# A six-stage encoder trunk in fp32 pairs: from hand-set orders and rooms to one list schedule over shared rooms

## The chip, the cores and the metric

The kernel runs on one core of a Trainium2 chip. The metric is the device time of one execution in microseconds (us). TensorE is called PE, VectorE DVE, ScalarE ACT, GpSimd POOL, and SyncE, which here only issues loads, SP.

## The reference

256 tokens of 1024 features go through two layers, each of three blocks with a residual and a layer norm: a gated feed-forward network (FFN, 2816 hidden), a mixer, and another FFN. The mixer of layer 0 is a bidirectional mLSTM with four heads, that of layer 1 windowed attention with 16 query heads and 4 key heads. Weights and data are float32.

```python
def swiglu(x, w_in, w_out):
    gu = x @ w_in
    g, u = gu[..., :D_FF], gu[..., D_FF:]
    return (jax.nn.silu(g) * u) @ w_out

def reference(x, ...):
    for l in range(DEPTH):
        x = layer_norm(ALPHA * x + 0.5 * swiglu(x, ffn_w_in[l, 0], ffn_w_out[l, 0]), ln_g[l, 0], ln_b[l, 0])
        j = l // N_MIXERS
        if l % N_MIXERS == 0:
            y = mlstm_mixer(x, ml_w_in[j], ml_gate_b[j], ml_norm_g[j], ml_w_out[j])
        else:
            y = window_attention(x, at_w_in[j], at_sink[j], at_w_out[j])
        x = layer_norm(ALPHA * x + y, ln_g[l, 1], ln_b[l, 1])
        x = layer_norm(ALPHA * x + 0.5 * swiglu(x, ffn_w_in[l, 1], ffn_w_out[l, 1]), ln_g[l, 2], ln_b[l, 2])
    return x
```

## The kernel before

Each float32 operand of a product is split into a rounded part (hi) and the rest (lo), and a product is three matmuls: hi x hi, hi x lo, lo x hi (`mm3`, L545). Weights come as raw words of 128 x 1024 (512 KB). ACT casts a word into `w_hi`, DVE subtracts that from the word into `w_lo`, and both lie in a ring of ten tiles (RING) until PE has used them. The normalized x is kept transposed in `xT`, also as hi and lo.

An FFN (`ffn`, L689) goes through its 2816 columns in this order: 512 columns by plain products, for which eight words stay in the ring while token half 0 and then token half 1 is multiplied (the first FFN takes both halves word by word); 256 columns from four words that hold gate and up side by side; two down rows (words of `w_out`, 12 matmuls each); and four groups (`seven`, L862) of 512 columns, in which seven block products stand in for eight, as in Strassen's scheme. A group uses sums of x blocks (S1 to S4), and sums of weight blocks that are made in place: DVE adds one raw word to another, and POOL issues a load that adds a block from memory onto a word (`Weights.transfer`, L305). Between the products stand further down rows, 16 in all by the end of the groups. `tail` (L644) then takes the last six rows, first all for token half 0 and then for half 1; `Norm` (L601) follows on DVE, with the power -0.5 on POOL; and `emit_x` (L685) transposes the new x on PE, for half 0 within the tail and for half 1 (`pending`) some matmuls into the next stage.

What sets the order. The instructions of each engine are written out in Python in their final order, and each engine works through its own queue strictly in order, with semaphores between the queues.

- PE's order is the program's.
- In the FFN stages the order of splits and sums on ACT and DVE comes from `Paced` (L56), which keeps an estimated clock for PE, DVE, ACT and the DMA, and from `Weights.fill` (L324), which is called after each matmul and emits a split when its word is expected to be in memory by 1 us before that (SOON). Elsewhere, and in the tails, tables of counts say how many splits go between which steps: RS, PU, MP, PD, TD. EX, LC and SW order other steps.
- Loads are issued on SP by `Weights.load` (L187), whenever a raw room becomes free. There are four rooms `w_raw` for all words; the words of the groups have eight rooms `s_raw0` to `s_raw3` and one `v_raw` in the pool of the stage. `Weights.open` (L179), called as an FFN begins (L812; in the first FFN at L808), declares these free, and the loads that fit go out at once.
- PSUM has eight banks, four named `pw` and four `py`.

The instructions of all engines but POOL are recorded by one helper (L142), so the profile gives that line for most of them; L108 and L106 are the loads.

Of the kernel before, what the change touches and what calls it, by code (L numbers as in the profile page):

```python
# [1 line left out]

# [14 lines left out]
D = 1024  # L17
# [7 lines left out]
RAW_BUFS = 4  # L25
S_RAW = 2
TAGS = ("w_raw", "s_raw0", "s_raw1", "s_raw2", "s_raw3")
V_RAW = 1
RING = 10
PU = [2, 0, 1, 2, 1, 2, 1, 1, 0, 1, 2, 4]  # L30
QC = [2, 12, 20, 28, 32]
SW = 1
FB = [1, 0, 1, 0, 2, 0, 0, 0, 1, 1, 2]
CT = [0, 1]
EX = [1, 2, 2, 2, 2, 2, 2, 2]
RS = [0, 0, 1, 0, 1, 0, 0, 0, 0, 0, 0, 3, 0, 0, 1, 0, 1, 0, 1, 0, 0, 0, 2, 0, 0, 0, 1, 0, 1, 2, 0, 0, 0, 1, 0, 0, 2, 0, 1, 1, 0, 0, 0, 0, 2, 2, 0, 1]
XP = [4, 0, 1, 2]
LC = [0, 0, 0, 0, 0, 1]
TD = [2, 3, 2, 0, 2, 1]
MP = [1, 0, 0, 0, 1, 0, 1, 1, 0, 0, 0, 0, 2, 2, 2]  # L40
PD = [7, 0, 6, 6, 5]
PEND = [6, 4, 6, 6, 6]


AHEAD = 300.0
SOON = -1000.0
NEAR = -700.0
LOOK = 6
LANDING = 2200.0
LOADING = 1340.0  # L50
SECOND = 1250.0
ADDING = 7000.0
SHARE = 2500.0


class Paced:  # L56

    def __init__(self, nc):  # L60
        self.nc = nc
        self.pe = self.vec = self.act = self.dma = 0.0
        self.there, self.places = {}, {}
        self.filler, self.alone = None, True
        self.vector = Engine(nc.vector, self.on_vector)
        self.scalar = Engine(nc.scalar, self.on_scalar)
        self.tensor = Engine(nc.tensor, self.on_tensor)

    def __getattr__(self, name):
        return getattr(self.nc, name)  # L70

    def place(self, ap):

        f = ap.ap[0][0]
        key = (ap.offset % f if f else 0, tuple(ap.ap[1:]))
        if key not in self.places:
            i = np.array([key[0]])
            for step, n in key[1]:
                i = (i[:, None] + step * np.arange(n if step else 1)[None, :]).reshape(-1)
            self.places[key] = i  # L80
        return self.places[key]

    def when(self, *aps):
        t = 0.0
        for ap in aps:
            a = self.there.get(ap.name)
            if a is not None:
                i = self.place(ap)
                t = max(t, a[i[i < a.size]].max(initial=0.0))
        return t  # L90

    def mark(self, ap, t):
        i = self.place(ap)
        a = self.there.get(ap.name)
        if a is None or a.size <= i.max():
            self.there[ap.name] = np.zeros(int(i.max()) + 1)
            if a is not None:
                self.there[ap.name][:a.size] = a
        self.there[ap.name][i] = t

    def load(self, ap, source, engine=None):
        if engine is not None:
            engine.dma_start(ap, source)
        elif isinstance(source, list):
            for k, src in enumerate(source):
                self.nc.sync.dma_start(ap[:, k].rearrange("p (m f) -> p m f", m=src.shape[1]), src)  # L106
        else:
            self.nc.sync.dma_start(ap, source)  # L108
        come = self.pe + LANDING
        alone, self.alone = self.alone, come > self.dma  # L110
        self.dma = max(self.dma, come) + LOADING + (SECOND if alone and not self.alone else 0.0)
        self.mark(ap, self.dma)

    def on_vector(self, name, n, out, ins):
        self.vec = max(self.vec, self.when(*ins)) + (n + 71) / 0.96
        for o in out:
            self.mark(o, self.vec + 115)

    def on_scalar(self, name, n, out, ins):
# [1394 lines left out]
```

## Time and profile before

| | before |
|---|---|
| device time, median of 3 runs | 935.05 us |
| lowest and highest run | 929.75, 936.56 us |
| span of the profiled execution | 940.3 us |
| instructions | 12583 |
| moved by DMA | 208.53 MB |

The profiled execution has no time of its own beside its span, which runs from its first to its last instruction; it is 5.25 us longer than the median of the runs. In the profile a matmul's busy time includes the time in which it is on its way through the array, so that neighbours overlap; the interval between the starts of two matmuls says how fast PE goes. A row of a table of windows gives start and end, length, busy time and count for PE, its weight loads (PEld), DVE, ACT and POOL, the granted clock of PE, the share of time in which the DMA engines were busy, and GB/s. A row of the chain of waits gives start, length, and the work on which the end of the program hung in that time. "Idle before" names the last instruction that a waiting one waited for.

### The profile page before, as it was taken

How to read it: one execution, taken by the hardware profiler on the slowest of the kernel's cores; microseconds unless marked ns; L12 is line 12 of the kernel's file. 1: busy time of each engine (PE TensorE's matmuls, PEld its weight loads, DVE VectorE, ACT ScalarE, POOL GpSimd, SP SyncE). 2: the span in 40 equal slices, each digit the busy share in tenths (PEclk: the TensorE clock that was granted, in tenths of full speed). 3: DMA queues.
4: the chain of work that ended last, by engine and by line, in shares of the span. 5: the costliest groups of instructions: out<-in, count | busy, mean ns of one | idle time of the engine just before them, and what ended most of it. 6: DMA issues, size and time to landing. Idle time of an engine off the chain costs nothing.

```text
span 940.3 us, 12583 instructions
## 1 busy us (share of the span) xinstructions
PE 915.2 (97%) x4459; PEld 758.6 (81%) x4459; DVE 804.3 (86%) x969; ACT 569.1 (61%) x793; POOL 155.2 (17%) x194
## 2 busy tenths in 40 slices
PE   9999999999999999999999899999999999999997
PEld 7777878789988877887777688887888887888885
DVE  5879999986799798899985999998868887889996
ACT  5566666446674465756634667665569564767670
POOL 0111122013211011111111112120445301111110
PEclk9999999999999999999999999999999998999999
DMA  8999997755635979897759699978434388898871
GB/s 272 343 248 278 259 264 189 254 157 172 210 110 162 354 194 297 251 221 222 215 192 355 149 280 273 262 177 246 161 135 135 93 270 265 248 240 252 227 197 45
DMA packets 100703, 208.53 MB, mean 222 GB/s; under 512 B 6904, under 2 KB 21264, under 8 KB 100640
## 3 DMA queue, kind: packets, MB, share of 16 engines
q1 hardware_dynamic: 82368, 173.04, 52.5%
q0 software_dynamic: 17696, 33.65, 21.4%
q10 hardware_dynamic: 576, 1.05, 0.3%
q8 instruction: 35, 0.57, 0.2%
q14 instruction: 28, 0.23, 0.1%
HBM read 206.65 MB, written 1.05 MB: 221 GB/s over the span
## 4 chain that ended last, share of the span: by engine, by line
PE 56%; DVE 17%; DMA 16%; issue 6%; ACT 4%; POOL 1%; SPq 1%; DVEq 0%; ACTq 0%; POOLq 0%
PE pw L142 35%; PE py L142 21%; DVE w_lo L142 9%; DMA s_raw<-in_ffn_w_in_dram 7%; DMA w_raw<-in_ffn_w_out_dram 4%; DMA w_raw<-in_ffn_w_in_dram 3%; ACT w_hi L142 2%; DVE s_raw L142 2%; DVE x L142 1%; DVE e L142 1%; DVE h_lo L142 1%; DVE stats L142 1%; DMA w_raw<-in_ml_w_in_dram 1%; DMA w_raw<-in_at_w_in_dram 1%; DVE h L142 1%
## 5 line engine op out<-in xcount | busy, mean ns | idle before, releaser
L142 DVE TENSOR_TENSOR w_lo<-w_raw,w_hi 128x1024 fp32r<-128x1024 f32 (+1 forms) x213 | 254.2, 1219 | 32.7 <-ACT w_hi L142 30.4
L142 ACT CAST w_hi<-w_raw 128x1024 fp32r<-128x1024 f32 (+1 forms) x213 | 217.0, 1047 | 90.0 <-DMA w_raw<-in_ffn_w_in_dram 43.2
L142 DVE TENSOR_TENSOR w_lo<-s_raw,w_hi 128x1024 fp32r<-128x1024 f32 x192 | 227.2, 1221 | 29.2 <-ACT w_hi L142 29.1
L142 ACT CAST w_hi<-s_raw 128x1024 fp32r<-128x1024 f32 x192 | 195.0, 1052 | 81.9 <-DVE s_raw L142 43.9
L142 PE MATMUL pw<-w_hi,xT_hi 128*128 128x512 f32 x480 | 189.7, 397 | 1.0 <-DVE e L142 1.0
L142 PE MATMUL pw<-w_lo,xT_hi 128*128 128x512 f32 x480 | 186.7, 390 | 1.5 <-DVE w_lo L142 1.5
L142 PE MATMUL pw<-w_hi,xT_lo 128*128 128x512 f32 x480 | 187.0, 391 | 0.8 <-DVE xT_lo L142 0.8
L308 POOL DMA_DIRECT2D s_raw<-in_ffn_w_in_dram x64 | 77.8, 1232 | 519.0 <-DVE s_raw L142 187.8
L142 PE MATMUL py<-w_hi,h_hi 128*128 128x512 f32 x349 | 140.9, 404 | 7.8 <-ACT h_hi L142 5.4
L142 PE MATMUL py<-w_hi,h_lo 128*128 128x512 f32 x349 | 138.9, 398 | 3.2 <-DVE h_lo L142 2.9
L142 PE MATMUL py<-w_lo,h_hi 128*128 128x512 f32 x349 | 137.5, 394 | 0.8 <-DVE w_lo L142 0.8
L142 PEld LDWEIGHTS pw<-w_lo,xT_hi 128*128 128x128 f32 x480 | 90.3, 188 | 20.6 <-DVE w_lo L142 3.0
L142 PEld LDWEIGHTS pw<-w_hi,xT_lo 128*128 128x128 f32 x480 | 90.0, 188 | 20.5 <-DVE xT_lo L142 1.4
L142 PEld LDWEIGHTS pw<-w_hi,xT_hi 128*128 128x128 f32 x480 | 90.0, 188 | 19.5 <-DVE e L142 1.2
L142 PE MATMUL pw<-w_lo,S_hi 128*128 128x512 f32 x256 | 99.8, 390 | 0.4 <-DVE w_lo L142 0.4
L142 PE MATMUL pw<-w_hi,S_hi 128*128 128x512 f32 x256 | 99.7, 390 | 0.4 <-ACT e L142 0.4
L142 PE MATMUL pw<-w_hi,S_lo 128*128 128x512 f32 x256 | 99.6, 389 | 0.0
L142 PEld LDWEIGHTS py<-w_hi,h_hi 128*128 128x128 f32 x349 | 66.5, 190 | 23.6 <-ACT h_hi L142 8.9
L142 PEld LDWEIGHTS py<-w_hi,h_lo 128*128 128x128 f32 x349 | 66.4, 190 | 21.4 <-DVE h_lo L142 7.3
L142 PEld LDWEIGHTS py<-w_lo,h_hi 128*128 128x128 f32 x349 | 66.7, 191 | 14.1 <-DVE w_lo L142 1.1
L142 DVE TENSOR_TENSOR s_raw<-s_raw,s_raw 128x1024 f32<-128x1024 f32 x64 | 76.4, 1219 | 1.1 <-DMA s_raw<-in_ffn_w_in_dram 1.1
L142 ACT COPY e<-pw 128x512 f32<-128x512 f32 x48 | 28.1, 586 | 58.4 <-PE pw L142 58.4
(205 smaller groups left out, 1154.1 us busy)
## 6 DMA issues: line engine op xcount, KB each, us to landing
s_raw<-in_ffn_w_in_dram SPq DMA_DIRECT2D x96, 512.0 KB, 8.2
w_raw<-in_ffn_w_out_dram SPq DMA_DIRECT2D x88, 512.0 KB, 6.5
w_raw<-in_ffn_w_in_dram SPq DMA_DIRECT2D x64, 512.0 KB, 6.8
s_raw<-in_ffn_w_in_dram POOLq DMA_DIRECT2D x64, 512.0 KB, 7.8
w_raw<-in_ml_w_in_dram SPq DMA_DIRECT2D x24, 512.0 KB, 4.6
w_raw<-in_ffn_w_in_dram SPq DMA_DIRECT2D x32, 256.0 KB, 3.5
w_raw<-in_at_w_in_dram SPq DMA_DIRECT2D x12, 512.0 KB, 4.6
w_raw<-in_ml_w_out_dram SPq DMA_DIRECT2D x8, 512.0 KB, 3.6
```

The lines of the kernel that those rows point to most:

```text
L142: r = f(out, *args, **kw)
L308: nc.gpsimd.dma_start(t.rearrange("p (k f) -> p k f", k=self.words[w]["k"]), source, accum_op=OP.add)
```

## The change

The program is no longer written out in its final order. It is noted step by step in plain order in a `Book`, over virtual tiles (`Room`, `View`) that have no place yet. The dependences follow from which parts of which tiles a step reads and writes. `cost` gives each step an estimated duration. `latest` gives each a due time: the time at which PE would need it if PE never waited, less the durations on the way there. `sequence` is the list schedule: it goes through time, and on each engine (SP's loads included) it takes, of the first 16 steps by due time, one that can start earliest, the earliest due among those within 1 ns. PE's steps keep their noted order. A step that opens a tile also needs a free room of its kind, and may not take one that an earlier noted tile needs. For loads there is one estimated DMA server (1.5 us for a word, 3 us for an accumulation), and SP does not run more than 6 us ahead of it. `emit` then writes out each engine's order.

Rooms: ten for `w_hi` and ten for `w_lo` as before; 20 of 4128 bytes ("big") shared by all stages, for raw words, h, S3 and S4, LN rows and the mixers' tiles; two "wide", for S1 and S2, the mLSTM's h or the attention's v; six of 2 KB; 20 small ones; and eight banks without the division in `pw` and `py`. The pools of the stages are gone, and so are `Paced`, `Weights` and the tables RS, PU, MP, PD, TD, EX, LC and SW. The arithmetic, the matmuls and their order, and the bytes that are loaded stay.

```diff
-RAW_BUFS = 4
-S_RAW = 2
...
-V_RAW = 1
-RING = 10
-PU = [2, 0, 1, 2, 1, 2, 1, 1, 0, 1, 2, 4]
...
+HOMES = {
+    "hi": (4096, 10),
+    "lo": (4096, 10),
+    "big": (4128, 20),
+    "wide": (4352, 2),
+    "temp": (2048, 6),
+    "small": (80, 20),
+    "bank": (2048, 8),
+    "const": (1 << 20, 1 << 20),
+}
...
+ISSUE = 600.0
+LANDING = 2200.0
+LOADING = 1500.0
+ADDING = 5500.0
+SHARE = 3000.0
+DEPTH_NS = 6000.0
...
-class Paced:
...
-class Weights:
...
+class Book:
...
+    def latest(self):
+        steps = self.steps
+        extra = [[] for _ in steps]
+        for kind, rooms in self.rooms.items():
+            held, free = [], HOMES[kind][1]
+            for r in rooms:
+                if free:
+                    free -= 1
+                else:
+                    held.sort(key=lambda x: x.last)
+                    old = held.pop(0)
+                    assert old.last < r.first, ("no room", kind, r.name, [x.name for x in held])
+                    for s in old.steps:
+                        extra[s.n].append(r.first)
+                held.append(r)
+        t = 0.0
+        for s in steps:
+            if s.engine == "PE":
+                s.due = t
+                t += s.takes
+        for s in reversed(steps):
+            if s.engine == "PE":
+                continue
+            after = s.later + s.takes
+            if s.name == "dma_start":
+                after += ADDING + LANDING if s.kw.get("accum_op") is not None else LANDING + LOADING
+            s.due = min([steps[d].due for d in [*s.succ, *extra[s.n]]], default=t + 5000.0) - after
+
+    def sequence(self):
+        steps = self.steps
+        state = {}
+        for kind, rooms in self.rooms.items():
+            first, last = np.array([r.first for r in rooms] or [0]), np.array([r.last for r in rooms] or [0])
+            n = len(rooms)
+            seq = np.array([int(((first[:k + 1] <= first[k]) & (last[:k + 1] >= first[k])).sum()) for k in range(n)] or [0])
+            cap = HOMES[kind][1]
+            assert seq.max() <= cap, (kind, seq.max(), cap)
+            state[kind] = dict(seq=seq.copy(), open=np.ones(max(n, 1), bool), cap=cap, free=[(0.0, j) for j in range(cap)])
+        self.state = state
+        waiting = [len(s.deps) for s in steps]
+        ready = [0.0] * len(steps)
+        todo = {e: [] for e in ("PE", "DVE", "ACT", "POOL", "SP")}
+        line = [s.n for s in steps if s.engine == "PE"]
+        at = 0
+        for s in steps:
+            if not waiting[s.n] and s.engine != "PE":
+                todo[s.engine].append(s.n)
+        for e in todo:
+            todo[e].sort(key=lambda n: steps[n].due)
+        free = {e: 0.0 for e in todo}
+        dma = 0.0
+        given = []
+
+        def homes(s, now):
+
+            need = {}
+            for r in s.rooms:
+                if r.slot is None:
+                    need.setdefault(r.kind, []).append(r)
+            t = now
+            for kind, rs in need.items():
+                st = state[kind]
+                if len(st["free"]) < len(rs):
+                    return None
+                for j, r in enumerate(rs):
+                    k = r.nth
+                    if k and (st["seq"][:k][st["open"][:k]] + j + 1 > st["cap"]).any():
+                        return None
+                t = max(t, sorted(st["free"])[len(rs) - 1][0])
+            return t
+
+        while len(given) < len(steps):
+            best = None
+            for e, list_ in todo.items():
+                if e == "PE":
+                    if at == len(line) or waiting[line[at]]:
+                        continue
+                    cands = [line[at]]
+                else:
+                    cands = list_[:16]
+                times = []
+                for n in cands:
+                    s = steps[n]
+                    t = max(free[e], ready[n])
+                    if e == "SP":
+                        t = max(t, dma - DEPTH_NS)
+                    t = homes(s, t)
+                    if t is not None:
+                        times.append((t, s.due, n))
+                if not times:
+                    continue
+                soon = min(times)[0] + 1.0
+                pick = min((x for x in times if x[0] <= soon), key=lambda x: x[1])
+                if best is None or pick[0] < best[0]:
+                    best = (*pick, e)
+            assert best is not None, "stuck"
+            t, _, n, e = best
+            s = steps[n]
+            s.start, s.end = t, t + s.takes
+            s.lands = s.end + s.later
+            if s.name == "dma_start":
+                if s.kw.get("accum_op") is not None:
+                    dma = max(dma, s.end) + SHARE
+                    s.lands = s.end + LANDING + ADDING
+                else:
+                    dma = max(dma, s.end + LANDING) + LOADING * min(1.0, np.prod(s.args[0].shape) / (128 * D))
+                    s.lands = dma
+            free[e] = s.end
+            if e == "PE":
+                at += 1
+            else:
+                todo[e].remove(n)
+            given.append(s)
+            for r in s.rooms:
+                if r.kind == "const":
+                    continue
+                st = state[r.kind]
+                if r.slot is None:
+                    st["free"].sort()
+                    r.slot = st["free"].pop(0)[1]
+                    st["open"][r.nth] = False
+                    st["seq"][:r.nth] += 1
+                r.left -= 1
+                r.until = max(r.until, s.lands)
+                if not r.left:
+                    st["free"].append((r.until, r.slot))
+                    st["seq"][:r.nth] -= 1
+            for d in s.succ:
+                waiting[d] -= 1
+                ready[d] = max(ready[d], s.end if steps[d].engine == e and s.name != "dma_start" else s.lands)
+                if not waiting[d] and steps[d].engine != "PE":
+                    list_ = todo[steps[d].engine]
+                    k = 0
+                    while k < len(list_) and steps[list_[k]].due <= steps[d].due:
+                        k += 1
+                    list_.insert(k, d)
+        self.given = given
+
+    def emit(self):
+        nc = self.nc
+        engines = {"PE": nc.tensor, "DVE": nc.vector, "ACT": nc.scalar, "POOL": nc.gpsimd, "SP": nc.sync}
+        real = lambda x: x.real() if isinstance(x, View) else x
+        for s in self.order():
+            for r in s.rooms:
+                if r.real is None:
+                    pool = self.pools[r.kind == "bank"]
+                    r.real = pool.tile(list(r.shape), r.dtype, name=r.name, tag=f"{r.kind}{r.slot}", bufs=1)
+            getattr(engines[s.engine], s.name)(*[real(x) for x in s.args], **{k: real(x) for k, x in s.kw.items()})
...
+    def word(src, k, name="raw"):
+        t = nc.tile(name, (128, D), "big")
+        if isinstance(src, list):
+            for j, one in enumerate(src):
+                nc.sync.dma_start(t.rearrange("p (k f) -> p k f", k=k)[:, j].rearrange("p (m f) -> p m f", m=one.shape[1]), one)
+        else:
+            nc.sync.dma_start(t.rearrange("p (k f) -> p k f", k=k), src)
+        return t, k
+
+    def split(w, scale=None, halves=False):
+        raw, k = w
+        hi, lo = nc.tile("w_hi", (128, D), "hi", FR), nc.tile("w_lo", (128, D), "lo", FR)
+        for s_ in (slice(0, 512), slice(512, D)) if halves else (A,):
+            if scale is None:
+                nc.scalar.copy(hi[:, s_], raw[:, s_])
+                nc.vector.tensor_sub(lo[:, s_], raw[:, s_], hi[:, s_].bitcast(F32))
+            else:
+                nc.scalar.activation(hi, raw, AF.Copy, scale=scale)
+                nc.vector.scalar_tensor_tensor(lo, raw, scale, hi.bitcast(F32), op0=OP.mult, op1=OP.subtract)
+        return hi.rearrange("p (k f) -> p k f", k=k), lo.rearrange("p (k f) -> p k f", k=k)
...
-                W.open(pool, ends[bound[0]])
...
+            b11 = [word(x_, 2, "b11") for x_ in at(0, c0)]
+            b12 = [word(x_, 2, "b12") for x_ in at(0, c1)]
+
+            def add(a, b):
+                nc.vector.tensor_add(a[0], a[0], b[0])
+
+            def bring(a, src):
+                nc.gpsimd.dma_start(a[0].rearrange("p (k f) -> p k f", k=2), src, accum_op=OP.add)
+
+            def then(w, *more):
+                def make():
+                    parts = split(w)
+                    for f_, a, b in more:
+                        f_(a, b)
+                    return parts
+                return make
+
+            product(qa, of(0, 0), [then(b11[j], (add, b11[j], b12[j]), (bring, b12[j], at(512, c1)[j])) for j in range(2)], True)
+            g0 = copied(qa, "e1")
+            before()
+            product(qc, of(4, 0), [lambda j=j: split(word(at(512, c0)[j], 2, "b21")) for j in range(2)], True)
+            nc.vector.tensor_add(g0, g0, qc)
+            down(1)
+            b22 = [word(x_, 2, "b22") for x_ in at(512, c1)]
+            qb = bank()
+            product(qb, sum_("S1"), [then(b11[j], (add, b11[j], b22[j])) for j in range(2)], True)
+            u1 = copied(qb, "e5")
+            product(qa, sum_("S2"), [then(b11[j], (bring, b11[j], at(512, c0)[j])) for j in range(2)], False)
+            u0 = copied(qa, "e2")
+            nc.scalar.activation(g0, g0, AF.Silu)
+            down(1)
+            product(qa, sum_("S3"), [then(b12[j]) for j in range(2)], False)
...
     pending()
+    nc.emit()
```

More of the change, by code (lines that the diff above doesn't have):

```diff
@@ L56 @@
-class Paced:
[L60 to L67, printed above, removed]
-    def __getattr__(self, name):
[L70 to L83, printed above, removed]
-        t = 0.0
[L85 to L119, printed above, removed]
-        self.act = max(self.act, self.when(*ins)) + n * 0.912 + 25
-        for o in out:
-            self.mark(o, self.act + 125)
-    def on_tensor(self, name, n, out, ins):
-        self.pe = max(self.pe, self.when(*ins)) + (109.0 if name == "transpose" else n / 2.4 + 13.3)
-        for o in out:
-            self.mark(o, self.pe + 200)
-        if self.filler is not None:
-            self.filler()
```

1887 lines of the change are left out of this document (818 added, 1069 removed).

## The prediction

> **What bounds the kernel now.** I read the engine totals first, then the table of windows by stage, then finer windows where TensorE loses time, then the chain of waits and the load queue just ahead of those places. In the engine totals PE stands out; the second number after it is its share of the span.
>
> ```profile
> span 940.3 us, 12583 instructions
> ...
> PE 915.2 (97%) x4459; PEld 758.6 (81%) x4459; DVE 804.3 (86%) x969; ACT 569.1 (61%) x793; POOL 155.2 (17%) x194
> ```
>
> PE idles for 940.3 - 915.2 = 25.1 us in all. The change keeps every matmul, so little more than that can be gained. The windows by stage (start:end, length, busy time of PE, PEld, DVE, ACT, POOL, the granted clock, DMA share, GB/s; the six rows are FFN, mLSTM, FFN, FFN, attention, FFN) show where the idle time lies.
>
> ```profile
> 0.00:175.00 175.00, 168.01 (x757) 136.51 (x757) 149.34 (x154) 113.17 (x137) 24.92 (x31) 1.00 0.90 264
> 175.00:300.00 125.00, 124.77 (x718) 108.96 (x719) 104.64 (x165) 69.99 (x123) 25.27 (x32) 1.00 0.54 175
> 300.00:479.00 179.00, 177.42 (x802) 144.19 (x801) 158.32 (x166) 110.70 (x134) 22.52 (x18) 1.00 0.83 244
> 479.00:655.00 176.00, 170.28 (x767) 139.60 (x766) 152.28 (x158) 108.00 (x130) 20.82 (x17) 0.99 0.84 240
> 655.00:753.00 98.00, 96.56 (x620) 82.81 (x619) 80.12 (x156) 62.77 (x147) 38.92 (x77) 1.00 0.42 140
> 753.00:940.30 187.30, 178.20 (x804) 146.57 (x802) 159.60 (x176) 104.43 (x126) 22.74 (x19) 0.97 0.74 218
> ```
>
> Idle by stage: 7.0, 0.2, 1.6, 5.7, 1.4 and 9.1 us. The three large ones are FFN stages. Inside a running group of seven products there is no loss at all:
>
> ```profile
> 571.00:602.00 31.00, 31.00 (x143) 25.64 (x142) 28.76 (x29) 20.53 (x25) 4.81 (x4) 1.00 0.92 262
> ```
>
> PE is busy 31.00 of 31.00 us, DVE 28.76: PE is the bound, DVE stands 7% below it. So the loss sits ahead of the groups. Finer windows of the last two FFN stages, and the chain's row for 24 matmuls in a row, which gives the price of one (5.44 / 24 = 0.2267 us):
>
> ```profile
> 515.00:520.00 5.00, 1.32 (x6) 0.75 (x4) 2.52 (x4) 3.26 (x5) 1.20 (x1) 1.00 0.94 228
> 520.00:525.00 5.00, 3.81 (x9) 2.39 (x10) 5.00 (x8) 3.16 (x6) 0.00 (x0) 0.66 0.69 220
> ...
> 785.00:790.00 5.00, 3.46 (x16) 2.53 (x14) 3.48 (x4) 3.46 (x6) 0.00 (x0) 1.00 1.09 290
> 790.00:795.00 5.00, 4.39 (x10) 3.06 (x11) 5.00 (x9) 2.21 (x5) 0.00 (x0) 0.59 0.85 283
> 795.00:800.00 5.00, 5.00 (x18) 3.90 (x17) 5.00 (x5) 3.05 (x3) 0.47 (x1) 0.73 0.00 0
> ```
> ```profile
> 597.80 5.44 PE pw L142 x24
> ```
>
> Five microseconds hold 22 matmuls of this size. From 515 to 525 there are 15 instead of 44: 29 x 0.2267 = 6.6 us lost. From 785 to 800 there are 44 instead of 66: 5.0 us lost. Part is waiting, part a lower granted clock (0.66, 0.59, 0.73) right after. The chain of waits names the cause, and the load queue (SP) shows how it arose:
>
> ```profile
> 502.57 13.21 DMA w_raw<-in_ffn_w_out_dram
> ```
> ```profile
> 773.21 11.61 DMA w_raw<-in_ffn_w_out_dram
> ```
> ```profile
> 490.02 8.37 SPq L108 DMA_DIRECT2D s_raw<-in_ffn_w_in_dram  x8
> ...
> 502.57 10.85 SPq L108 DMA_DIRECT2D w_raw<-in_ffn_w_out_dram  x4
> ```
>
> The rooms s_raw belong to the stage's own pool. When it opens, eight of their loads go out at once at 490, although the first product that uses them comes only after two down rows, and the down rows (w_out) queued behind them take 13.21 us. Just before, the DMA engines had room to spare (0.68 and 0.73 of their time), because only four w_raw rooms were there to load into:
>
> ```profile
> 460.00:480.00 20.00, 19.65 (x92) 15.12 (x89) 17.46 (x22) 9.12 (x12) 1.46 (x1) 1.00 0.68 224
> 480.00:500.00 20.00, 19.38 (x91) 16.15 (x92) 16.50 (x20) 9.72 (x13) 1.46 (x1) 1.00 0.73 237
> ```
>
> **The change, part by part.** *Loads.* The split ring stays at ten tiles. Raw words lose their fixed rooms (4 + 8 + 1 = 13 in an FFN, 4 outside the groups) and share 20 with the stage's other 4 KB tiles. In a group two h pairs, the pair of 256 and S3, S4 hold 7, which leaves 13 again; at a boundary, where the groups' words are used up, 20 less two h pairs and two LN rows leave 14 instead of 4. SP's order goes by due time, so that rows are no longer behind words used later. The free DMA time in the two rows above is (0.32 + 0.27) x 20 = 11.8 us, near the 13.21 us by which the rows were late. I therefore count both stalls as gone but for 0.4 us each, the idle that the middle FFN shows at this place without a stall:
>
> ```profile
> 320.00:340.00 20.00, 19.65 (x88) 15.74 (x87) 16.96 (x21) 9.56 (x14) 2.57 (x2) 1.00 1.03 334
> ```
>
> That is -6.2 us (FFN 3) and -4.6 us (FFN 4). The first FFN has the same burst of eight, at 23.67 us, and idles 1.86 + 1.18 + 0.52 = 3.6 us from 40 to 100:
>
> ```profile
> 23.67 6.59 SPq L108 DMA_DIRECT2D s_raw<-in_ffn_w_in_dram  x8
> ```
> ```profile
> 40.00:60.00 20.00, 18.14 (x78) 13.88 (x77) 12.83 (x14) 10.82 (x14) 2.00 (x2) 1.00 0.92 278
> 60.00:80.00 20.00, 18.82 (x82) 14.92 (x82) 17.83 (x19) 14.75 (x17) 2.42 (x3) 1.00 0.97 295
> 80.00:100.00 20.00, 19.48 (x90) 15.71 (x89) 20.00 (x20) 12.76 (x17) 3.61 (x3) 1.00 0.86 200
> ```
>
> DMA is at 0.92 to 0.97 here, so not all can go: between 0 and -3.6 us I take -3.0, nearer the full amount because the new rooms can be filled from the first load on, and over the whole stage DMA has a tenth of its time left (0.90 in the first row by stage).
>
> *What late there comes next.* With the rows in time, PE runs into the first group behind DVE, which must make S1 to S4 and the splits; its 5.00 of 5.00 us from 520 to 525 are that work being caught up.
>
> *Matmuls, splits, casts.* Same number and size, and the PE order is the noted one, which repeats the old: 0. *Instructions on POOL and the accumulating loads:* the same 64 issues, still behind the sums that they wait for: 0 while the ring hides them (a rival below). *Start and tail.* The first matmul waits for ident, and the last adds and stores follow the last matmul: same code, 0.
>
> *Order of DVE and ACT.* The hand-set counts of splits between steps (RS, PU, MP, PD, TD, EX, LC) are replaced by a list schedule that starts whatever can start first, by due time among those. It knows no margin (the old planner asked for words to be in 1 us early), and it never holds an engine free for a step about to become ready. What that costs has its nearest rows at a stage's end, in the chain of waits around 475:
>
> ```profile
> 473.60 1.47 POOL rs L628
> ...
> 476.30 2.35 DVE w_lo L142 x2
> 478.65 0.61 DVE x L142
> ...
> 479.97 0.60 DVE xT_lo L142
> 480.62 9.37 PE pw L142 x40
> ```
>
> PE starts the next stage at 480.62, when xT_lo is done; the two splits at 476.30 stand in that way already. Each hop between engines (PE to the norm, POOL's power back to DVE, ACT's xT_hi to xT_lo) can meet one split on DVE, and ACT's copy one cast:
>
> ```profile
> L142 DVE TENSOR_TENSOR w_lo<-w_raw,w_hi 128x1024 fp32r<-128x1024 f32 (+1 forms) x213 | 254.2, 1219 | 32.7 <-ACT w_hi L142 30.4
> L142 ACT CAST w_hi<-w_raw 128x1024 fp32r<-128x1024 f32 (+1 forms) x213 | 217.0, 1047 | 90.0 <-DMA w_raw<-in_ffn_w_in_dram 43.2
> ```
>
> At worst 3 x 1.22 + 1.05 = 4.7 us at each of five boundaries, 23.5 us; at best the idle of the three quiet stages goes, 0.2 + 1.6 + 1.4 = 3.2 us. I take +1.0, near the lower end: during the last six down rows six of the ten ring slots are held, so DVE often has no split to start, and due times put the norm first among what is ready.
>
> Sum: -6.2 - 4.6 - 3.0 + 1.0 = -12.8 us, from 940.3 us to 927.5 us in a profile like this one. The span shown stands 5.25 us above the median of 935.05 us (the runs go from 929.75 to 936.56); the same difference from the median gives 922.3 us.
>
> **A rule against the trace.** These rows are TensorE's own around the last stall.
>
> ```profile
> 790.13 0.50 PE L142 MATMUL py<-w_hi,h_hi 128*128 128x512 f32 x1 [1.67 <-DVE w_lo L142]
> 790.47 0.40 PE L142 MATMUL py<-w_lo,h_hi 128*128 128x512 f32 x1
> 791.34 0.80 PE L142 MATMUL py<-w_hi,h_lo 128*128 128x512 f32 x1 [0.47 <-DVE h_lo L142]
> ```
>
> PE waited 1.67 + 0.47 = 2.14 us, and 5.0 us were lost. The Trainium skill, "TensorE: Matmul & The Clock Gate", the section on the clock gate, has the clock halved after an idle window of about 3.4 us. By that rule this stall, with no idle stretch so long, would have cost its 2.14 us alone, and the sum would be 2.9 us smaller, 925.2 us. The trace does not agree: the clock fell to 0.59 after it, and I go by the trace.
>
> **Rivals.** *Slower: splits in the way of the norm.* The worst case above comes true at all five boundaries, and two of these stalls bring the slow clock, at 5.0 - 2.14 = 2.9 us each. Time: 935.05 - 13.8 + 23.5 + 5.8 = 950.6 us. For it speaks that xT_lo already ends last at 480.62, so any delay there reaches PE at once; against it the held ring slots. It decides once a boundary loses over 13.8 / 5 = 2.8 us.
>
> *Slower: accumulating loads later than planned.* The new schedule counts 1.25 + 2.2 + 5.5 = 8.95 us from issue to landing. From 540 to 640 they took:
>
> ```profile
> DMA to landing us min/median/max: 5.6/7.4/12.2
> ```
>
> One at 12.2 us comes 3.25 us late, and an engine that reads its queue in order stands still for that. Two such waits in each group cost 6.5 us of DVE against 31.00 - 28.76 = 2.2 us to spare, so 4.3 us a group, 69 us over 16 groups. Ten tiles of lead, of 18 used in 31 us, are 17 us in each of four FFNs, 68 us: just enough. Were the lead only half, 69 - 34 = 35 us would show: 935.05 - 13.8 + 35 = 956 us. For it speaks that more loads lie in the hardware queue at once; against it the median of 7.4. The Trainium skill, "DMA: Bandwidth & Descriptors", the section on queues and rings, says that each DMA engine takes turns between the rows with work, which would lengthen an accumulation beside a fuller load queue. The trace neither agrees nor disagrees, since the loads that lay beside each are not told apart.
>
> *No difference.* The schedule plans the DMA wrongly where it is fullest, the rows still come late, or what is won there is lost at the boundaries: 935 us, inside 925.7 to 944.4.
>
> **How the numbers follow.** The forecast holds 0.50, the norm rival 0.22, the accumulation rival 0.11, no difference 0.17. The forecast's own range goes from 911 (6.6 + 5.0 + 3.6 + 3.2 = 18.4 us gone, from the lowest run's 929.75) to 926. About 1% is what a measurement of this kernel can tell from no change. The range to 958 takes in both slower cases at their prices, and 911 to 958 leaves out some 0.04 below and 0.14 above. Faster 0.50, same 0.17, slower 0.33.
>
> **What would show it.** Right: PE idle of 14 us or less outside start and tail; no chain piece of over 10 us on w_out rows; in the FFN starts the group words' loads mixed with rows; granted clock 1.00 all the way. The norm rival: PE idle of 3 us and more ahead of each xT, ended by DVE. The accumulation rival: PE idle inside the groups, with ACT waiting for the accumulated words. Most likely to break the forecast is a wait of PE on DVE's order in a place that no row of before shows.

## The result: 0.7% slower, and the profile after

| | before | after |
|---|---|---|
| device time, median of 13 runs | 936.21 us | 942.10 us |
| lowest and highest run | 929.75, 943.40 us | 941.13, 943.80 us |
| span of the profiled execution | 940.3 us | 940.0 us |

The ratio is 1.0068, with a 95% interval of 1.0048 to 1.0089. (One run after the change, of 1138.44 us, was disturbed; the lowest and highest run and the ratio leave it out.) The time is inside the range of the prediction, 20 us above its forecast. The profiled execution of before was one of its longer ones, that of after an ordinary one, so that the spans hide the difference.

The first lines of the page after, and the table of windows by stage:

```profile
span 940.0 us, 12633 instructions
...
PE 919.6 (98%) x4459; PEld 756.4 (80%) x4459; DVE 809.6 (86%) x969; ACT 584.0 (62%) x793; POOL 155.6 (17%) x194
```
```profile
0.00:175.00 175.00, 171.43 (x772) 139.37 (x773) 157.11 (x164) 120.62 (x143) 34.05 (x62) 1.00 0.95 285
175.00:300.00 125.00, 123.85 (x710) 106.75 (x709) 99.48 (x157) 69.52 (x118) 21.94 (x25) 1.00 0.60 204
300.00:479.00 179.00, 178.46 (x800) 144.59 (x799) 161.57 (x169) 114.72 (x134) 22.32 (x18) 1.00 0.84 241
479.00:655.00 176.00, 176.00 (x792) 143.24 (x791) 158.97 (x165) 112.06 (x132) 23.48 (x20) 1.00 0.84 245
655.00:753.00 98.00, 90.93 (x586) 76.98 (x585) 70.71 (x142) 61.25 (x144) 30.98 (x50) 1.00 0.41 125
753.00:940.00 187.00, 178.89 (x808) 145.46 (x806) 161.75 (x177) 105.85 (x125) 22.80 (x19) 0.99 0.66 185
```

PE now idles 3.6, 1.2, 0.5, 0.0, 7.1 and 8.1 us by stage. The stalls of the FFNs went as forecast, and the granted clock stays at 1.00 (0.99 in the last stage, where it falls only after PE's last matmul). The attention, the fifth row, idles 7.1 us, where it idled 1.4 before. In all PE idles 20.4 us, less than the 25.1 before, and yet the kernel is slower: busy time can't say whether the work itself became slower. The places of the old stalls and the running group show that it did:

```profile
515.00:520.00 5.00, 5.00 (x23) 4.08 (x22) 3.10 (x4) 1.86 (x2) 2.22 (x2) 1.00 0.56 79
520.00:525.00 5.00, 5.00 (x26) 4.05 (x25) 3.96 (x4) 4.25 (x6) 0.18 (x1) 1.00 1.10 208
785.00:790.00 5.00, 5.00 (x23) 4.01 (x23) 4.83 (x6) 2.33 (x4) 1.21 (x1) 1.00 0.95 218
790.00:795.00 5.00, 5.00 (x23) 4.08 (x22) 4.42 (x7) 2.38 (x3) 1.20 (x1) 1.00 0.75 137
795.00:800.00 5.00, 5.00 (x25) 4.07 (x24) 2.92 (x3) 3.33 (x4) 1.19 (x1) 1.00 0.94 142
...
571.00:602.00 31.00, 31.00 (x140) 25.30 (x139) 29.54 (x30) 21.70 (x26) 4.81 (x4) 1.00 0.95 272
```

PE is busy all the time in each of these rows, but from 571 to 602 it goes through 140 matmuls where it went through 143. The chain of waits gives the price. A row for 24 matmuls of 512 columns, which was 5.44 us before, is now:

```profile
513.54 5.56 PE py L434 x24
```

That is 5.56 / 24 = 231.7 ns in place of 226.7 ns for a matmul of the same size. Over all intervals between the starts of two matmuls of 512 columns in a row, those of 300 ns and more (waits, slow clock) left out, the trace has a mean of 231.7 ns, against 227.5 ns before. The program has some 3450 of them, so an estimate is 4.2 x 3450 = 14.5 us, at one and the same clock. The prediction had set it at nothing.

### The profile page after: what moved, and what is told of

It is laid out like the page before. It is cut to its first block, busy times and chain, and to the rows that moved or that the text cites. A ratio compares the mean times of both kernels' runs of the same rounds, so it can differ in the third digit from the quotient of the medians.

```text
span 940.0 us, 12633 instructions
## 1 busy us (share of the span) xinstructions
PE 919.6 (98%) x4459; PEld 756.4 (80%) x4459; DVE 809.6 (86%) x969; ACT 584.0 (62%) x793; POOL 155.6 (17%) x194
## 4 chain that ended last, share of the span: by engine, by line
PE 84%; DVE 8%; DMA 3%; issue 2%; ACT 2%; POOL 1%; DVEq 0%; SPq 0%; ACTq 0%; POOLq 0%
PE pw L434 56%; PE py L434 27%; DVE w_lo L434 4%; DMA raw<-in_ffn_w_in_dram 1%; DMA raw<-in_ml_w_in_dram 1%; DVE x L434 1%; ACT w_hi L434 1%; ACT sc L434 1%; DMA raw<-in_ffn_w_out_dram 0%; POOL rs L434 0%; DVE stats L434 0%; DVE b L434 0%; DVE xT_lo L434 0%; DVE sc L434 0%; DVE e L434 0%
## 5 line engine op out<-in xcount | busy, mean ns | idle before, releaser
L434 ACT CAST w_hi<-b 128x1024 fp32r<-128x1024 f32 x224 | 234.1, 1053 | 93.5 <-PE py L434 53.4
L434 DVE TENSOR_TENSOR w_lo<-b,w_hi 128x1024 fp32r<-128x1024 f32 x224 | 267.5, 1219 | 25.4 <-ACT w_hi L434 25.2
L434 ACT CAST w_hi<-raw 128x1024 fp32r<-128x1024 f32 (+1 forms) x181 | 186.8, 1046 | 101.5 <-PE py L434 65.9
L434 DVE TENSOR_TENSOR w_lo<-raw,w_hi 128x1024 fp32r<-128x1024 f32 (+1 forms) x181 | 216.8, 1214 | 33.8 <-ACT w_hi L434 33.3
L434 PE MATMUL pw<-w_hi,S 128*128 128x512 f32 x512 | 164.6, 392 | 0.0
L434 POOL DMA_DIRECT2D b<-in_ffn_w_in_dram x64 | 77.3, 1210 | 465.9 <-DVE b L434 161.4
L434 PEld LDWEIGHTS pw<-w_hi,S 128*128 128x128 f32 x512 | 96.1, 188 | 21.7
L434 PE MATMUL pw<-w_lo,S 128*128 128x512 f32 x256 | 100.4, 392 | 0.0
L434 DVE TENSOR_TENSOR b<-b,b 128x1024 f32<-128x1024 f32 x64 | 78.0, 1221 | 1.2
L434 PEld LDWEIGHTS pw<-w_lo,S 128*128 128x128 f32 x256 | 48.1, 188 | 10.9
```

The source lines that it names most:

```text
L434: getattr(engines[s.engine], s.name)(*[real(x) for x in s.args], **{k: real(x) for k, x in s.kw.items()})
```

## What differs: the place of the operands

The longer intervals come with every bank (means of 231.2 to 232.0 ns by bank, 227.1 to 228.3 before), and whatever lies beside them: 231.7 ns where DVE and ACT are both busy, 231.4 ns where neither is. They follow where the tiles lie. In the compiled program of before, 3997 of the 4459 pairs of stationary operand (that of the weight load) and moving operand (here of 512 columns in most) begin at the same place modulo 256 bytes; after, 1385 do. `xT` is now allocated ahead of the small constants (its place moved by 32 bytes), and the list schedule puts tiles into rooms of up to 4128 and 80 bytes, which shift what lies behind them by 32, 64 and more. In the trace of the changed kernel itself the interval is 228.4 ns where a matmul and both its neighbours have their operands at the same place (655 of them), and 232.9 ns where none of the three has (1694). Two theories were put to the test: that the place sets the interval, and that the company does (more DVE, ACT and DMA work beside each matmul). A third said that only some shifts cost.

### m_align: the place alone

Chains of 36 matmuls of 512 columns, with nothing beside them, in one execution, with the stationary and the moving data shifted by given numbers of bytes.

```diff
+CASES = [("za", 0, 0), ("sb", 32, 0), ("sc", 64, 0), ("sd", 96, 0), ("se", 128, 0), ("sf", 160, 0), ("sg", 192, 0),
+         ("sh", 224, 0), ("mb", 0, 32), ("mc", 0, 64), ("me", 0, 128), ("bb", 32, 32), ("bc", 64, 64), ("be", 128, 128),
+         ("zz", 0, 0)]
```

> Theory 1 (address classes): a matmul of 512 columns starts every 227 ns while its two operands start at the same place within 256 bytes, and every 231 to 235 ns where they do not. This kernel computes nothing of the reference (its output is a copy of x); it runs chains of 36 matmuls with nothing beside them, for 15 pairs of offsets. Expected by theory 1: sums za, zz, bb, bc, be at 227 ns, and sb to sh and mb to me at 231 ns or more. Theory 2 (company: the shared rooms set the data that PE reads among data that other engines and loads write): all 15 at 227 ns, as nothing else runs. Theory 3 (only a shift by 32 bytes within 64 costs): sc, se, sg, mc, me at 227 ns too.

In the chain of waits each chain of 36 is a row (start, length). Names that begin with s have the stationary data shifted, with m the moving data, with b both alike; zz has none shifted.

```profile
47.82 8.67 PE sb L50 x36
...
76.05 8.68 PE sc L50 x36
...
132.60 8.67 PE se L50 x36
...
179.66 8.54 PE sg L50 x36
...
235.69 8.68 PE mb L50 x36
...
273.48 8.53 PE mc L50 x36
...
329.36 8.49 PE bb L50 x36
...
412.37 8.47 PE zz L50 x36
```

Shifted together (bb) a chain takes as long as without a shift (zz), 8.47 to 8.49 us. Shifted apart by 32, 64 or 128 bytes it takes 8.67 to 8.68: 0.20 us over 35 intervals, 5.7 ns each. Only where the stationary data lie 192 bytes further, or, what is the same modulo 256, the moving data 64 (sg, mc), is it 1.7 ns, an exception that theory 1 had not expected. So it is the difference of the two places that counts, and the theory of the place holds with no company at all. The third theory falls as far as multiples of 64 were held to be free.

### a_xt and a_pad: the changed kernel with its operands put back

a_xt creates `xt` and `xT` after the small constants again. a_pad moreover fills the shared rooms up to multiples of 256 bytes; one room of 4128 bytes and the small rooms, which are not filled up, now lie behind the others. Order, waits and the other neighbours stay.

```diff
@@ a_xt
-    xt = [const(f"x{t}", [128, D]) for t in range(2)]
-    xT = tuple(const("xT" + e, [128, 8, S], FR) for e in ("_hi", "_lo"))
...
+    xt = [const(f"x{t}", [128, D]) for t in range(2)]
+    xT = tuple(const("xT" + e, [128, 8, S], FR) for e in ("_hi", "_lo"))
@@ a_pad, in emit
+        odd = [x for x, n in most.items() if n == 1032][-1]
+        for (kind, slot), n in [*[x for x in most.items() if x[0] != odd], (odd, 1024)]:
+            self.pools[0].tile([128, -(-n // 64) * 64], F32, name="pad", tag=f"{kind}{slot}", bufs=1)
```

> The changed kernel with xT made after the small constants, so that it starts at byte 96 of 256 like the weight ring instead of 128; all rooms, orders and waits as they were. Theory 1: the some 1500 matmuls on xT go from 232.9 ns to 228 to 230 ns, the time from 942.1 us to 934 to 938 us. Theories 2 and 3 in the form that the rooms' company or the new order slows the matmuls: no change, 942 us.

> The changed kernel with xT moved as in the run before, and every shared room padded to a multiple of 256 bytes, so that all operands of the 3447 matmuls of 512 columns start at byte 96 of 256; which room lies beside which, orders and waits as they were. Theory 1: the mean interval falls from 231.7 to 227.5 ns, 14 us in all: 928 us. Theory 2 (company): the rooms lie among each other as before, so 942 us.

| | pairs at the same place, of 4459 | mean interval | median time | ratio to before |
|---|---|---|---|---|
| after | 1385 | 231.7 ns | 942.10 us | 1.0068 [1.0048, 1.0089] |
| a_xt | 2927 | 230.2 ns | 938.39 us | 1.0026 [1.0005, 1.0047] |
| a_pad | 4033 | 227.5 ns | 929.91 us | 0.9932 [0.9912, 0.9952] |

The chain of a_pad, at the same 24 matmuls:

```profile
506.51 5.44 PE py L443 x24
```

It is 5.44 us again, as before the change. The time falls by 12.2 us in two steps, in the order of the intervals, while the work beside the matmuls stays: the theory of the company is refuted. The sizes are a little short of theory 1, with a_xt just above its 934 to 938 us and a_pad 1.9 us above its 928. With this alone the change is 0.7% faster than before, not 0.7% slower.

### b_xt32: the kernel before, shifted

The other way round: 32 bytes put in front of `xT` in the kernel before (and 224 behind, so that the rest stays).

```diff
+    state.tile([128, 8], F32, name="pad_a", tag="pad_a")
...
+    state.tile([128, 56], F32, name="pad_b", tag="pad_b")
```

> The kernel before with 32 bytes ahead of xT and 224 behind it, so that xT alone starts at byte 128 of 256 while the weights stay at 96. Theory 1: the some 1500 matmuls on xT go from 227.6 to about 233 ns, the time from 936 to about 943 us. Theories 2 and 3 (company, new order): no change, 936 us.

937.16 us, ratio 1.0002 [0.9972, 1.0031]: a miss. The intervals of the matmuls with `xT` did rise from 228 to 233 ns, the mean from 227.5 to 229.9, which is 2.4 x 3450 = 8 us of matmul time, but the device time did not rise by more than the 3 us that the interval leaves open. The windows of b_xt32 where the kernel before stalled hint at the reason:

```profile
500.00:520.00 20.00, 17.17 (x75) 13.28 (x73) 13.43 (x17) 8.91 (x12) 2.42 (x2) 1.00 1.03 325
...
780.00:800.00 20.00, 18.94 (x82) 14.62 (x81) 16.07 (x19) 12.70 (x18) 3.60 (x3) 1.00 0.69 191
```

From 780 to 800 there are 82 matmuls at clock 1.00, where the kernel before has 17.86 us busy with 67 at 0.83. The rows of `w_out` come when they come; a PE that arrives later waits less for them. If that is so, the shift must cost time once the stalls are gone.

## The stalls of the kernel before

### b_open and b_open32

b_open takes half of the burst of eight loads away from the start of an FFN (all but the first), with the rooms of the kernel before: one room for each tag at first, the second after the first down row. b_open32 adds the 32 bytes of b_xt32.

```diff
+    def more(self):
+        for tag in TAGS[1:]:
+            self.free[tag] += 1
+        self.load()
...
-                W.open(pool, ends[bound[0]])
+                W.open(pool, ends[bound[0]], s_raw=1)
...
             down(1)
+            if not start:
+                W.more()
```

> The kernel before, with one room instead of two for each of the four tags of the groups' words when an FFN (but the first) opens, and the other four rooms opened after the first down row: the burst at the FFN's start is four loads of group words instead of eight, so that the rows behind it are issued some 4 x 1.5 = 6 us earlier. Theory 'burst' (the prediction's cause of the stalls, that the new schedule removes): PE's idle time from 500 to 540 and from 780 to 800 falls by 4 to 9 us together with the slow clock behind it, and the time falls by 4 to 11 us, to 925 to 932 us. Rival 'rooms': the rows wait for one of the four w_raw rooms and not for the queue, or the group words now come late themselves, and the time stays within 2 us of the kernel before.

> The kernel b_open (931.21 us; the kernel before with half the burst of loads, its stalls at the starts of the FFNs mostly gone), with xT moved by 32 bytes as in b_xt32, so that 1536 of its 4459 pairs of matmul operands no longer begin at the same place modulo 256 bytes. Theory 'the stalls hid it': in b_xt32 slower matmuls cost no time because the loads were late at the FFN's start anyhow; with these stalls gone the 5 to 6 ns of each of some 1400 matmuls show: 5 to 9 us more than b_open, 936 to 940 us. Rival 'the place costs little by itself in this order of work': 931 to 934 us; then the cost of the place in the changed kernel would need another reason.

b_open takes 931.21 us, ratio 0.9950 [0.9932, 0.9968], 4.9 us less than before in the same comparison: the burst was a cause, at the lower end of what was expected. The windows of b_open:

```profile
500.00:520.00 20.00, 20.00 (x91) 16.54 (x90) 18.20 (x23) 12.79 (x18) 1.21 (x1) 1.00 0.99 337
520.00:540.00 20.00, 19.29 (x87) 15.61 (x86) 15.81 (x16) 12.68 (x16) 3.61 (x3) 1.00 0.88 224
...
780.00:800.00 20.00, 20.00 (x92) 16.55 (x91) 15.97 (x19) 11.95 (x16) 2.41 (x2) 1.00 0.96 273
800.00:820.00 20.00, 18.48 (x82) 14.69 (x81) 18.28 (x19) 12.66 (x16) 3.58 (x3) 1.00 0.99 265
```

The stalls at 515 and 785 are gone, with the slow clock behind them (PE idles 0.7 us from 500 to 540 and from 780 to 800, where it idled 7.0); some of the loss returns 20 us later, because the group's words now come late themselves. PE's waits in b_open (sum, times, longest) say so:

```profile
PE pw L142 <- DVE w_lo L142: 9.1, 8, 2.1
```

Before, these were 2.0 us in 3 waits. The new schedule, which changes rooms and order, shows no stall at these places and a single wait on `w_lo`, of 1.3 us. That speaks for the rooms mattering beside the order, but the two were not tried apart in it.

b_open32 takes 936.08 us, ratio 0.9998 [0.9972, 1.0025], 4.9 us more than b_open by the medians and 4.5 us by the ratios, whose intervals don't overlap. That is just under the 5 to 9 us expected, and nearer to it than to the rival's 3 us at most. The 8 us of slower matmuls, which cost nothing that could be measured beside the full stalls, cost 4.5 to 4.9 us beside what is left of them. That the rest is hidden by the waits left in b_open is argued only.

## The attention

PE's waits from 655 to 760 in the kernel after; before there were 1.4 us in this stretch.

```profile
PE pw L434 <- DVE nm L434: 4.9, 7, 1.0
PE pw L434 <- DVE xT_lo L434: 1.7, 2, 1.1
PE pw L434 <- DVE q_lo L434: 1.0, 1, 1.0
PE py L434 <- DVE qd L434: 0.5, 1, 0.5
```

`nm` is the minimum that DVE's reduce takes of a score. The timelines of PE and DVE in a_pad, at one such wait:

```profile
694.48 0.28 PE L443 MATMUL pw<-kT_lo,q_hi 64*128 64x256 f32 x2
694.60 0.28 PE L443 MATMUL pw<-kT_hi,q_lo 64*128 64x256 f32 x2
694.71 0.28 PE L443 MATMUL pw<-kT_hi,q_hi 64*128 64x256 f32 x2
695.81 0.39 PE L443 MATMUL pw<-kT_lo,q_hi 64*128 64x256 f32 x2 [0.82 <-DVE nm L443]
```
```profile
693.80 1.23 DVE L443 TENSOR_TENSOR w_lo<-raw,w_hi 128x1024 fp32r<-128x1024 f32 x1 [0.45 <-ACT w_hi L443]
694.94 0.42 DVE L443 TENSOR_TENSOR q_lo<-pw,q_hi 128x256 fp32r<-128x256 f32 x1
695.27 0.47 DVE L443 CUSTOM_DVE_ANT_0 sc<-pw,dist,neg_sink 128x256 f32<-128x256 f32 x1
```

PE stops in the middle of a group: the second half of the bank (the token half 1) is begun, and then PE waits until DVE has read the first half. The `Book` knows a dependence only where elements overlap, so its schedule puts the reduce of one half between the matmuls of the other, and the wait is then set for the bank as a whole. The Trainium skill, "PSUM — Partial Sum Buffer", the section on bank collisions, asks for semaphores by bank and not by address; the program's waits follow that, as the 0.82 us above show, and the schedule did not plan with it. Before, all reduces of a group came behind all its matmuls.

DVE comes to the reduce late here because of a weight split that itself waited for ACT's cast. Two edits were tried in turn on a_pad.

### a_bank, a_cost, a_half: two edits of the schedule

a_bank lets the reduce depend on all matmuls into its bank. a_cost, on top of it, brings five durations nearer to what these timelines of a_pad on ACT and POOL show, and has 18 small rooms in place of 20:

```profile
690.51 0.51 ACT L443 ACTIVATE sc<-sc,nm 128x256 f32<-128x256 f32 x1
690.92 0.19 ACT L443 ACTIVATION_READ_ACCUMULATOR sc<-sc,nm 128x1 f32 x1
691.01 0.50 ACT L443 ACTIVATE sc<-sc,nm 128x256 f32<-128x256 f32 x1
...
692.00 0.47 ACT L443 ACTIVATE es<-nm,sink 128x2 f32<-128x2 f32 x2
```
```profile
692.55 0.20 POOL L443 TENSOR_TENSOR sm<-sm,es 128x4 f32<-128x4 f32 x1 [3.26 <-ACT es L443]
692.83 1.02 POOL L443 TENSOR_TENSOR sm<-sm,minus_one 128x4 f32<-128x4 f32 x1
693.95 2.79 POOL L443 TENSOR_SCALAR sc<-sc,sm 128x256 f32<-128x256 f32 x4
```

An exponential starts 0.50 us after the one before; `cost` says 388 ns. Two small ones (`es`) take 0.47 us together; `cost` says 57 ns each. On POOL the sum of four columns takes 0.20 us and their power 1.02 us, where `cost` says 1.0 and 1.5 us; the four scalings take 2.79 us; `cost` says 4 x 298 ns. a_half is a_cost without the edit of a_bank, and a_cost2 is a_cost once more, beside it.

```diff
@@ a_bank, in note
+            if name == "tensor_tensor_reduce" and r.kind == "bank":
+                i = A
...
-                s.deps.update(r.writer[p, i].tolist())
+                s.deps.update(np.ravel(r.writer[p, i]).tolist())
@@ a_cost, in cost
             if "accum_out" in s.kw:
-                s.takes += 100.0
+                s.takes += 200.0
+            elif n <= 4:
+                s.takes = 185.0
...
+            if s.name == "tensor_tensor" and n == 4:
+                s.takes = 1100.0
+            if s.name == "tensor_add" and n == 4:
+                s.takes = 280.0
+            if s.name == "tensor_scalar" and n == 256:
+                s.takes = 650.0
```

> The kernel with aligned rooms (a_pad, 929.91 us), in which each of the attention's tensor_tensor_reduce steps depends on all matmuls into its bank, not only on those into the half that it reads. In a_pad DVE takes the reduce of one half as soon as that half is written, and PE stops in the middle of the group, before the matmuls into the other half, until DVE has read: 4.7 us in 7 waits, up to 0.9 us each. Theory 'half a bank': the wait is between a reader of one half and a writer of the other, it exists because the schedule knows parts of a tile only; with the edit the waits of PE on DVE nm go (0 to 1 us left), PE's idle time from 655 to 753 falls from 7.9 us to 3 to 4 us, and the time falls by 3 to 5 us, to 925 to 927 us. Rival 'DVE and ACT are late in attention whatever the order': the reduces start when both halves are there, later than now, the next group's banks come free later, the waits move to other places, and the time stays within 1.5 us of 929.9.

> The kernel a_bank (928.49 us; aligned rooms, whole banks), in which four durations of the schedule in the attention follow the profile: an exponential with its sum 488 ns in place of 388, one of 2 columns 185 instead of 57, POOL's scaling of 256 columns 650 instead of 298, its power of 4 columns 1100 instead of 1500; 18 small rooms instead of 20, for the space. In a_bank the attention (655 to 753) idles 6.0 us on PE, in the kernel before 1.4 us. Theory 'durations': the schedule believes ACT some 0.65 us and POOL some 1 us a step faster than they are, puts casts of weights ahead of steps that PE then waits for, and with the right durations the idle time falls by 2 to 4.5 us, the time to 924 to 926.5 us. Rival 'no reservation': a list schedule starts whatever can start, whatever the durations, and the idle time stays within 1.5 us and the time within 1.5 us of a_bank.

> The kernel a_cost (925.01 us) without the edit of a_bank: the durations are the corrected ones, and a reduce in the attention again depends only on the matmuls into the half of the bank that it reads. Theory 'both count': the waits of PE on DVE nm come back (7 waits, 4 to 5 us), and the time rises by 1 to 4 us, to 926 to 929 us; this would show that a_bank's edit is worth something once DVE and ACT are planned rightly, though alone it gave 1.4 us with overlapping intervals. Rival 'the durations alone': with the right durations the reduces go where they do no harm, the waits on nm stay under 2 us, and the time stays within 1 us of 925.0.

> The kernel a_cost again, beside a_half on the same chip: 925.0 us within 1 us, and PE's idle time from 655 to 753 within 0.5 us of 4.0 us. There is no rival for this run; it gives the difference to a_half a common base.

| | edit | median (lowest, highest) | ratio to before |
|---|---|---|---|
| a_pad | | 929.91 (929.34, 931.17) | 0.9932 [0.9912, 0.9952] |
| a_bank | banks | 928.49 (927.80, 929.77) | 0.9919 [0.9892, 0.9946] |
| a_half | durations | 926.94 (926.43, 928.37) | 0.9893 [0.9867, 0.9918] |
| a_cost | both | 925.01 (924.51, 926.21) | 0.9891 [0.9856, 0.9927] |
| a_cost2 | both | 925.13 (924.80, 926.70) | 0.9873 [0.9846, 0.9900] |

a_bank alone is inconclusive: the waits on `nm` are gone, as its theory said, but others took their place (2.3 us on `q_lo`, 1.5 us on `pr`), PE's idle time from 655 to 753 fell from 7.9 to 6.0 us, and the time by 1.4 us with overlapping intervals. The theory of the durations holds: a_cost is 3.5 us below a_bank, the ranges of their runs do not meet (those of the ratios do), and the attention is at the row below. The two ran on different chips; by the ratios to the kernel before beside each, the difference is 2.6 us.

```profile
655.00:753.00 98.00, 94.03 (x608) 80.68 (x607) 72.91 (x145) 60.39 (x144) 30.72 (x50) 1.00 0.44 145
```

That is 4.0 us of idle time, 2.0 less than in a_bank. The rival, that a list schedule loses this whatever its durations, allowed 1.5 us at most, and falls. a_half shows that banks count too: on the same chip it is 1.8 us above a_cost2, no run of the one reaching the middle of the other, and its waits on `nm` are back, though 4 and not the 7 expected:

```profile
PE pw L451 <- DVE nm L451: 2.6, 4, 0.9
```

a_cost beats both kernels: 1.1 to 1.3% below before, 17 us below the change as it was. What is left of the attention's 4.0 us against 1.4 us before was not followed.

## Why the prediction was wrong, point by point

- **"Matmuls, splits, casts. Same number and size, and the PE order is the noted one, which repeats the old: 0."** This is the step that failed. Number, size and order are the same, but each matmul of 512 columns takes 4.2 ns longer, an estimated 14.5 us in all; a_pad took 12.2 us of that back by moving tiles and nothing else. In the prediction's own sum, -13.8 + 14.5 and, for the order of DVE and ACT, +5.7 make +6.4 us; 5.9 us were measured. The diff showed the cause to whoever asked where the operands lie: rooms of 4128 bytes, and `xT` created at another place. The prediction held the rooms against loads only. No row of before could have given the price, since in its trace all the matmuls behind the mean of 227.5 ns have their operands at the same place.
- **Order of DVE and ACT, +1.0 us.** Mis-sized: the attention's idle time alone rose by 5.7 us. The bound given, 23.5 us, was built from the five stage boundaries, and those held (waits on `xT_lo` at the starts of stages come to 3.2 us in all, against 0.8 before). The loss was inside the attention, from half banks and wrong durations, of which no row of before could warn; `cost` against the measured ACT and POOL rows could have. The prediction's last sentence named such a wait of PE on DVE as what would most likely break it; it came (4.9 us on `nm`), as the smaller part of the loss.
- **Stalls at the FFN starts, -6.2 and -4.6, and -3.0 in the first FFN.** Right. The fourth row by stage is busy for 176.00 of 176.00 us, the clock is 1.00, the longest piece of the chain on `w_out` is 4.59 us (13.21 before), and the first FFN idles 3.6 us in place of 7.0. By size: -13.8 us and the attention's 6.5 us in a_pad (1.4 to 7.9) make -7.3; a_pad against before is -5.9 us. The rows that gave the -13.8 come from a long execution: a span is 1.7 us shorter than its time (940.0 and 941.73 us in the kernel after), so that the profiled one stands some 7 us above the median, and not 5.25. How large the stalls were in an execution of median length was not looked at.
- **The burst as the stalls' cause.** Right in part: half the burst alone gives 4.9 us (b_open), with the rest moved to the group's words.
- **Accumulating loads, 0.** Right: inside the running group PE is busy for 31.00 of 31.00 us, and issue to landing has a median of 8.1 us over the kernel.
- **The rivals.** Neither the norm nor the accumulating loads were it. "No difference" has the time (942.1 in 925.7 to 944.4), but not the mechanism: what was won at the FFNs stayed won, and was lost elsewhere.
- **"What would show it right"** came true, all of it, and the kernel was slower: PE idles 11.7 us outside start and tail (1.7 and 7.0 us), the longest piece on `w_out` is short, loads of rows and group words alternate (seen from 457 to 485 us), and the clock is 1.00 until PE's last matmul. It asked for idle time only; the interval between two matmuls belonged beside it.
- **The clock and the rule.** Going by the trace was right. In a_bank the clock fell again, after a single wait of PE of 1.8 us, on `q_lo`:

```profile
690.00:700.00 10.00, 9.21 (x72) 7.81 (x72) 8.03 (x23) 8.32 (x25) 4.66 (x9) 1.00 0.34 106
700.00:710.00 10.00, 7.96 (x58) 6.52 (x57) 7.41 (x21) 7.25 (x23) 6.70 (x12) 0.94 0.18 54
710.00:720.00 10.00, 10.00 (x69) 8.61 (x69) 5.52 (x18) 7.17 (x24) 4.53 (x8) 0.89 0.18 60
```

  The sum of idle time doesn't decide it. The kernel after idles more here, 3.27 us from 680 to 700 (a_bank 2.83 us from 690 to 710), in waits of at most 1.0 us, and the clock stays:

```profile
680.00:700.00 20.00, 16.73 (x132) 14.23 (x131) 15.12 (x37) 13.14 (x34) 6.82 (x12) 1.00 0.30 85
```

  Nor does the longest wait alone: in b_open PE waited 1.90 us at 549 us, and the clock stayed at 1.00. The idle window of some 3.4 us in the Trainium skill, "TensorE: Matmul & The Clock Gate", the section on the clock gate, again doesn't fit as a threshold for one wait. What decides was not found.

## What to carry to other kernels

When a change moves tiles, compare where the two operands of each matmul begin, and after it the interval between two matmuls in a long row of the chain, not only PE's idle time. A list schedule is as good as the durations and dependences it is given: take the durations from starts in the profile, and let it depend on whole banks where the waits will be set by bank. Slower work ahead of a late load can cost nothing, so a part tried on a kernel that stalls says little of its price on one that doesn't.

## What the runs showed of the hardware

- A matmul of 512 columns with its weight load repeats every 227 ns when stationary and moving data begin at the same place modulo 256 bytes, some 233 ns at the other distances tried, and some 229 ns when the stationary data are 192 bytes ahead (m_align: 8.47, 8.68 and 8.54 us for 36). The granted clock in m_align was 1.00 throughout. Why the place counts was not found.
- Slower matmuls need not show: b_xt32 has an estimated 8 us more matmul time than before, and the same device time within 3 us.
